# Values turned by VectorE through memory instead of by TensorE, and three small transfers on GpSimd's queue

## The chip, the cores and the metric

The kernel runs on one core of one Trainium2 chip. The metric is device time in microseconds for one execution; the time given for a kernel is the median of its runs. TensorE is called PE in the profile, VectorE DVE, ScalarE ACT, GpSimd POOL, SyncE SP.

## The reference

One step of a small hybrid decoder trunk with two layers. Layer 0 projects 2048 features into the inputs of a gated delta rule (8 heads of 128x128, with a short convolution ahead) and of a gated linear attention, GLA (4 heads, keys of 128, values of 256), and projects their gated outputs back. Layer 1 is a gated linear recurrence (RG-LRU). 256 prompt tokens start from zero state; 64 sample tokens (8 sequences of 8) start from given states. All is float32.

```python
def _ab_mixer(x, S_a, conv_a, S_b, w_in, conv_w, a_log, dt_bias, norm_a, w_lr, b_lr, norm_b, w_out):
    proj = jnp.einsum('btd,de->bte', x, w_in)
    qkv, b_raw, a_raw, z_a, q_b, k_b, v_b, lr_b, z_b = jnp.split(proj, _ab_split_points(), axis=-1)
    qkv, new_conv_a = _causal_conv(qkv, conv_a, conv_w)
    ...
    o_a, S_a_new = _gated_delta_rule(q_a, k_a, v_a, g, beta, S_a)
    ...
    o_b, S_b_new = _gla(q_b, k_b, v_b, gk.reshape(B, T, H_B, DK_B), S_b)
    ...
    return jnp.einsum('bte,ed->btd', o, w_out), S_a_new, new_conv_a, S_b_new

def _gated_delta_rule(q, k, v, g, beta, S0):
    ...
    A = jnp.where(strict, jnp.einsum('nbhid,nbhjd->nbhij', kb, k) * decay, 0.0)
    rhs = jnp.concatenate([v * beta[..., None], kb * jnp.exp(G)[..., None]], axis=-1)
    sol = lax.linalg.triangular_solve(A + jnp.eye(C, dtype=jnp.float32), rhs,
                                      left_side=True, lower=True, unit_diagonal=True)
    ...

def _gla(q, k, v, gk, S0):
    ...
    intra = jnp.einsum('nbhij,nbhjv->nbhiv', A, v)
    def step(S, inp):
        qg_c, k_c, v_c, B_c, intra_c = inp
        o = jnp.einsum('bhck,bhkv->bhcv', qg_c, S) + intra_c
        ...
        S = S * jnp.exp(b_last)[..., None] + jnp.einsum('bhck,bhcv->bhkv', k_dec, v_c)
        return S, o
```

## The kernel before

The projections compute 512 output features at a time: a *group* is 8 weight chunks of 512 KB (tile wst, loaded by SP, line 219), each of two slices of 128 input features. The weights of a slice are split into two float32r parts, wh by ACT (line 253) and wl by DVE (line 254), and each 128x128 block is multiplied in three products of 128x320 (line 386; 320 tokens). A group's four results (f0 to f3) stand in four PSUM banks called acc and are evacuated at its end, mostly by DVE: into slab for the convolved groups (lines 489 and 490, then the taps yc, line 598, and the activation into the tile qkv), into zp and zs for the gates z (lines 1548 and 1549). The next group needs the banks again. The order of groups is Q0, K0, V0, V1, K1, Q1 (delta rule; two halves of four heads), QB, KB, VB0, VB1 (GLA), ZA, ZB, then the output projection (group 14 on) and layer 1.

All other work is written as generators that stand in queues (hi, lo, lo2, tails) and are advanced in *slots* between the products, 64 slots to a group; a table WAITS gives the slots that each generator lets pass at its yields. So the order on every engine is fixed when the kernel is built. A second table, HELD, ties pieces of the GLA sample to chosen products of group 14: key (group, number of the product block), value the pieces held behind it.

V comes out of the projection with features on partitions and is needed with tokens on partitions:

- quad_a prepares a *quad*, four heads of one prompt block of 128 tokens (two halves times two blocks, four prompt quads, and a fifth for the samples). It transposes V on PE (vt, line 791), and the result times bk becomes rv. rv is first used in quad_b, as the right side of the triangular solve. Beside it quad_a makes kt, qt, kk, kq, dtm, bt and mt. delta_half(half) runs quad_a for the two blocks, the inversion of 32x32 blocks, quad_front and quad_b.
- The GLA prompt transposes VB for each block and head, two at a time (gvt, line 1447), together with the keys (line 1448), copies all three to gvk by ACT (line 1450), and uses them in gpo (line 1454) and gsn (line 1458).

delta_sample is one chain for the 8 sequences: own (diagonal 8x8 blocks) is written to memory as bt_scratch (line 808), read as ab (line 857), inverted on DVE by pairs tmp and xi (lines 864 and 866), written to xt_scratch (line 870), read back as own (line 880), spread into XT (line 881) and multiplied with rv to y (line 1085). All four transfers are on SP's queue, between the weight loads. rv of the samples takes the states into account by pq (lines 1069, 1077).

The GLA sample multiplies four 1 MB states (st, loaded at line 1474) in two steps (gpo, line 1517, 32 products on two states each); the tile has three buffers, so the fourth state is loaded once the first step is done.

Of the kernel before, what the change touches and what calls it, by code (L numbers as in the profile page):

```python
# [7 lines left out]
F32 = mybir.dt.float32  # L8
F32R = mybir.dt.float32r
U32 = mybir.dt.uint32  # L10
AF = mybir.ActivationFunctionType
# [3 lines left out]
P = 128  # L15
# [20 lines left out]
NA0 = 2  # L36
# [4 lines left out]
HELD = {(14, 15): (3,), (14, 21): (0, 2), (14, 27): (4,), (14, 33): (1,)}  # L41
# [26 lines left out]
def wait(name):  # L68
    for _ in range(WAITS[name]):
        yield  # L70
# [3 lines left out]
def hybrid_step(ctx, tc, x_cols, x_rows, w_head, w_dense, w_small, w_lr, w_gate, par_a, par_b, par_c, gains, last_gain,  # L74
                head_rows, state_delta, state_gla,
                y_cols, p_delta, p_gla, s_delta, s_gla, dconv, lconv, lru_out):
    nc = tc.nc
# [8 lines left out]
    vk_d = nc.dram_tensor("vk_scratch", (2, 32, 4, 3 * P), F32, kind="Internal").ap()  # L86
    xt_d = nc.dram_tensor("xt_scratch", (4, 16, 8, 8), F32, kind="Internal").ap()
# [10 lines left out]
    def bank4(name):  # L98
        return psum.tile([P, 4, P], F32, name=name, tag="bg", bufs=4)
# [457 lines left out]
    def evac_conv_a(slot_name, half, part):  # L557
# [53 lines left out]
        def after():  # L611
            tails.append(conv_state_out(env["ws"], st["p"], dconv[:, st["ft"]:st["ft"] + 4, :]))
            if part == 2 and half == 0:
                hi.append(later(lambda: lo.append(delta_half(0))))
            if part == 0 and half == 1:
                hi.append(later(lambda: lo.extend([delta_half(1), delta_sample()])))
# [79 lines left out]
    def quad_prompt(half, c):  # L696
        q = Quad()
        q.U, q.n = 4, 32
        q.id = 8 * half + 4 * c
        cs = slice(c * P, (c + 1) * P)  # L700
        q.k = lambda u: env["K", half][:, u, cs]
        q.q = lambda u: env["Q", half][:, u, cs]
        q.v = lambda u: env["V", half][:, u, cs]
        q.qall = lambda: env["Q", half][:, :, cs]
        q.gc = c * 8 + half * 4
        q.um, q.sl, q.far = umask, sl_r, far
        q.late = c > 0
        q.on_tag, q.nbuf = "lg", 2
        return q
# [15 lines left out]
    def quad_a(q, ws, nbuf):  # L725
# [63 lines left out]
        ps = bank4("vt")  # L789
        for u in range(U):  # L790
            pe.transpose(ps[:, u, :], q.v(u), ident)
        q.rv = t("rv")
        scaled4(q.rv, ps, q.bk, NA0)
        yield from wait("quad_a.4")
# [54 lines left out]
    def invert(ws, n_units, n):  # L849
# [7 lines left out]
        sp.dma_start(ab, bt_d.rearrange("u b j i -> (u b) j i"))  # L857
        pool.memset(xi[:parts], 0.0)
        pool.memset(xi[:parts].rearrange("p i c -> p (i c)")[:, ::n + 1], 1.0)
        yield from wait("invert.1")  # L860
# [9 lines left out]
        sp.dma_start(xt_d.rearrange("u b c i -> (u b) c i"), xt)  # L870

    def load_inv(q, ws):
# [4 lines left out]
        else:  # L877
            q.xt = ws.tile([P, 4, P], F32, name="XT", tag="XT")
            own = ws.tile([P, 4, 8], F32, name="own", tag="own", bufs=1)
            q.read = sp.dma_start(own, xt_d.rearrange("u b c i -> (b c) u i"))  # L880
# [116 lines left out]
    def delta_half(half):  # L997
        with tc.tile_pool(name=f"gdn{half}", bufs=1, side="right", reuse_waits="tile") as ws:
# [14 lines left out]
            for p_ in pt:  # L1013
                pool.memset(p_, 0.0)
            yield from wait("quad_b.1")
# [6 lines left out]
    def delta_sample():  # L1022
# [3 lines left out]
        with tc.tile_pool(name="gdns", bufs=1, side="right", reuse_waits="tile") as ws:  # L1026
# [96 lines left out]
            for u in range(4):  # L1123
                to_rows(kt_d[u], q.ktm[:, u, :], P)
        env["done"].add("gdns")

    def to_rows(d, t, w):

        sp.dma_start(bass.AP(tensor=d.tensor, offset=d.offset, ap=[[w, 4], [4 * w, 32], [1, w]]), t)
# [143 lines left out]
    def evac_plain(tag, slot_name, idx, smp, scale=None):  # L1273
# [17 lines left out]
        def after():  # L1291
            env["done"].add((slot_name, idx))
        evac.late = late
        return None, evac, after

# [61 lines left out]
    def gla_head(h, ws, kept):  # L1357
# [74 lines left out]
        for c in range(2):  # L1432
# [12 lines left out]
            for hf in range(2):  # L1445
                vt = 2 * h + hf
                pe.transpose(pt[:, hf, :], env["VB", vt // 4][:, vt % 4, cs], ident)
            pe.transpose(pt[:, 2, :], kd[128][:, cs], ident)
            vk = t("gvk", [P, 3, P])
            act.activation(vk, pt[:, :3], AF.Copy)  # L1450
            yield from wait("gla.3")
            po = bank("gpo")
            vtm = vk[:, 0:2, :].rearrange("p a b -> p (a b)")
# [4 lines left out]
            pe.matmul(ps[:, :256], vk[:, 2, :], vtm, start=True, stop=True)  # L1458
# [670 lines left out]
```

## Time and profile before

| | us |
|---|---|
| median of 3 runs | 967.99 (966.45 to 969.25) |
| the profiled execution | 967.67 |
| its span in the trace | 965.9 |
| granted TensorE clock | 0.999 |
| busy: DVE, ACT, POOL | 684.0, 539.3, 125.6 |

Durations below come from the one profiled execution. A row of a group of instructions gives line, engine, operation, tile written and tiles read, count, and time. Matmuls overlap in the array, so their single durations are longer than the distance between them. In rows of a stretch the engines stand in the order PE, weight loads, DVE, ACT, POOL, with the number of instructions in brackets, then the granted clock, the DMA share and GB/s. In the chain of waits each row is start, duration, what. The DMA moved 175.14 MB, 181 GB/s on average:

```profile
DMA packets 66098, 175.14 MB, mean 181 GB/s; under 512 B 16264, under 2 KB 23688, under 8 KB 65496
q1 hardware_dynamic: 61384, 163.86, 53.2%
q0 software_dynamic: 2560, 8.65, 2.3%
```

q1 carries SP's transfers, q0 those that GpSimd issues.

### The profile page before, as it was taken

To read this page: it belongs to the slowest core of one execution; us is meant where nothing else is said; L and a number is where in the kernel's file an instruction comes from. 1 tells how busy PE (TensorE), PEld (TensorE's weight loads), DVE (VectorE), ACT (ScalarE), POOL (GpSimd) and SP (SyncE) were. 2 spreads that over 40 slices of the span, in tenths; PEclk is the share of its full clock that TensorE was granted. 3 is DMA by queue.
4 is the path that set the end of the run, shared out by engine and by line. 5 is a ranking of instruction groups with operands and counts; after the bars stand their busy time and mean duration, and the time that the engine had idled before them with its cause. 6 is when DMAs were issued, how large, how long until landed. Compare 5 with 4: busy or idle time off the path is not lost.

```text
span 965.9 us, 18747 instructions
## 1 busy us (share of the span) xinstructions
PE 954.4 (99%) x6946; PEld 940.1 (97%) x6946; DVE 684.0 (71%) x1509; ACT 539.3 (56%) x1094; POOL 125.6 (13%) x293
## 2 busy tenths in 40 slices
PE   9999999999999999999999999999999999999997
PEld 9999999999999998999989999999999999999996
DVE  7599887666545566789676778667969668865763
ACT  6767864457333444777434346338696885434452
POOL 3010108303280011121100000100000000000000
PEclk9999999999999999999999999999999999999999
DMA  9854454534554366444568776644436435587742
GB/s 325 286 176 139 134 146 149 151 109 124 156 157 144 108 221 204 159 137 116 211 231 312 239 242 209 226 150 151 157 122 189 132 118 178 191 274 263 252 156 109
DMA packets 66098, 175.14 MB, mean 181 GB/s; under 512 B 16264, under 2 KB 23688, under 8 KB 65496
## 3 DMA queue, kind: packets, MB, share of 16 engines
q1 hardware_dynamic: 61384, 163.86, 53.2%
q0 software_dynamic: 2560, 8.65, 2.3%
q10 hardware_dynamic: 2064, 1.45, 0.5%
q8 instruction: 54, 0.88, 0.4%
q14 instruction: 36, 0.29, 0.1%
HBM read 159.77 MB, written 14.16 MB: 180 GB/s over the span
## 4 chain that ended last, share of the span: by engine, by line
PE 96%; DMA 2%; DVE 1%; issue 0%; ACT 0%; SPq 0%; DVEq 0%
PE acc L386 83%; PE acc L273 3%; DMA st<-in_state_gla_dram 1%; PE fbt L316 1%; PE lg L1709 0%; PE lg L1708 0%; PE lg L1707 0%; PE kq L811 0%; PE kk L797 0%; PE usn L1201 0%; DMA xt_scratch<-ab 0%; PE gpo L1517 0%; PE po L978 0%; PE y L969 0%; DMA wst<-in_w_head_dram 0%; PE sn L983 0%
## 5 line engine op out<-in xcount | busy, mean ns | idle before, releaser
L386 PE MATMUL acc<-xh,wh 128*128 128x320 f32 x1856 | 581.3, 313 | 0.6 <-ACT wh L240 0.6
L386 PE MATMUL acc<-xl,wh 128*128 128x320 f32 x1856 | 574.0, 310 | 0.0
L386 PE MATMUL acc<-xh,wl 128*128 128x320 f32 x1856 | 573.9, 310 | 0.0
L253 ACT ACTIVATE wh<-wst 128x512 fp32r<-128x512 f32 x479 | 279.9, 623 | 300.1 <-PE acc L386 230.7
L254 DVE TENSOR_TENSOR wl<-wst,wh 128x512 fp32r<-128x512 f32 x479 | 317.6, 693 | 166.6 <-ACT wh L253 163.5
L386 PEld LDWEIGHTS acc<-xh,wh 128*128 128x128 f32 x1856 | 348.7, 188 | 3.2 <-issue 0.9
L386 PEld LDWEIGHTS acc<-xl,wh 128*128 128x128 f32 x1856 | 348.6, 188 | 0.5
L386 PEld LDWEIGHTS acc<-xh,wl 128*128 128x128 f32 x1856 | 348.3, 188 | 0.4 <-DVE wl L254 0.3
L598 DVE SCALAR_TENSOR_TENSOR yc<-slab,pa,yc 128x344 f32<-128x344 f32 x72 | 40.8, 579 | 1.7 <-ACT yc L102 1.5
L839 POOL TENSOR_TENSOR tmp<-ab,xi 128x60 f32<-128x60 f32 (+24 forms) x62 | 23.9, 386 | 55.7 <-DMA ab<-bd_scratch 51.1
L841 POOL TENSOR_TENSOR xi<-xi,tmp 128x60 f32<-128x60 f32 (+24 forms) x62 | 25.5, 411 | 4.9
L1231 POOL DMA_DIRECT2D out_s_delta_dram<-ust x8 | 5.9, 742 | 102.8 <-DVE ust L1228 102.8
L1265 POOL DMA_DIRECT2D out_s_gla_dram<-ugt x8 | 4.3, 542 | 113.5 <-DVE ugt L1262 113.5
L273 PE MATMUL acc<-xl,wh 128*128 128x320 f32 (+1 forms) x64 | 18.7, 292 | 0.0
L273 PE MATMUL acc<-xh,wl 128*128 128x320 f32 (+1 forms) x64 | 18.7, 292 | 0.0
L273 PE MATMUL acc<-xh,wh 128*128 128x320 f32 (+1 forms) x64 | 18.6, 291 | 0.0
L602 ACT ACTIVATE qkv<-yc 128x256 f32<-128x256 f32 x24 | 9.9, 414 | 15.2 <-DVE yc L598 15.2
L1228 DVE SCALAR_TENSOR_TENSOR ust<-ust,es,usn 128x128 f32<-128x128 f32 x64 | 18.3, 345 | 0.1
L1667 DVE SCALAR_TENSOR_TENSOR yc<-slab,pb,yc 128x344 f32<-128x344 f32 x32 | 17.4, 576 | 0.7 <-ACT yc L1665 0.5
L489 DVE TENSOR_TENSOR slab<-acc,rb 128x256 f32<-128x256 f32 x36 | 15.0, 418 | 3.3 <-PE acc L386 3.0
L1736 POOL MEMSET aa<- 128x32 f32 x4 | 0.7, 166 | 120.9 <-ACT rr L1723 66.2
L102 ACT ACTIVATE yc<-slab,pa 128x344 f32<-128x344 f32 x24 | 13.7, 577 | 4.8 <-DVE slab L490 4.5
(468 smaller groups left out, 990.2 us busy)
## 6 DMA issues: line engine op xcount, KB each, us to landing
wst<-in_w_dense_dram SPq DMA_DIRECT2D x237, 512.0 KB, 3.7
st<-in_state_delta_dram SPq DMA_DIRECT2D x8, 512.0 KB, 5.8
st<-in_state_gla_dram SPq DMA_DIRECT2D x4, 1024.0 KB, 5.8
ust<-in_state_delta_dram SPq DMA_DIRECT2D x8, 512.0 KB, 5.9
out_s_delta_dram<-ust POOLq DMA_DIRECT2D x8, 512.0 KB, 6.5
ugt<-in_state_gla_dram SPq DMA_DIRECT2D x8, 512.0 KB, 5.0
out_s_gla_dram<-ugt POOLq DMA_DIRECT2D x8, 512.0 KB, 4.1
xtok<-in_x_rows_dram SPq DMA_DIRECT2D x6, 512.0 KB, 7.3
```

What stands on the lines that cost most here:

```text
L102: return act.activation(out, in_, AF.Identity, scale=scale)
L253: act.activation(h, wst[i][:, a, :], AF.Copy)
L254: env["last_split"] = dve.tensor_sub(l, wst[i][:, a, :], h.bitcast(F32))
L273: mm = pe.matmul(accs[f][:, cols], w[:, fs], x[:, cols], start=(k == 0 and j == 0), stop=(k == KT - 1 and j == 2), skip_group_check=True)
L386: mm = pe.matmul(o, (h, h, l)[j][:, fs], (xh, xl, xh)[j][k], start=(k == 0 and j == 0), stop=(k == KT - 1 and j == 2))
L489: dve.tensor_mul(xp[:, 3:259], xp[:, 3:259] if acc is None else acc[:, :256], rb[:, :256])
L598: dve.scalar_tensor_tensor(y[:, :n], xp[:, j:j + n], pa[:, ft, j:j + 1], y[:, :n], op0=OP.mult, op1=OP.add)
L602: act.activation(st["t"][:, f, :], y[:, :TP], AF.Silu)
L839: behind(pool.tensor_mul(tv, ab[:, j, j + 1:, None].to_broadcast([P, m, w]), xi[:, j:j + 1, :w].to_broadcast([P, m, w])))
L841: behind(pool.tensor_add(xi[:, j + 1:, :w], xi[:, j + 1:, :w], tv))
L1228: dve.scalar_tensor_tensor(s_, s_, es[:, col:col + 1], ps[b][:, r, :], op0=OP.mult, op1=OP.add)
L1667: dve.scalar_tensor_tensor(y[:, :n], xp[:, j:j + n], pb[:, ft, 2 + j:3 + j], y[:, :n], op0=OP.mult, op1=OP.add)
```

## The change

Four things change.

1. V of both halves and VB of both halves are turned by a new generator, turn: four DVE stream transposes (of 32x32 blocks) into the buffer ob[3], one write of 512 KB to vt_scratch, two reads of 256 KB back into the tile that V came from, all on SP. turned gives the view of the result, in which the 256 or 512 numbers of a token lie in runs of 32. The prompt quads make rv in delta_half just ahead of quad_front, after waiting for the flag ("V", half); the samples keep their PE transposes. The GLA reads VB through the same view, and ACT copies only the keys.
2. The read of bt_scratch, the write of xt_scratch and the read of own in delta_sample are issued by GpSimd; the write of bt_scratch stays on SP. The kt_scratch writes are ordered behind the read of own.
3. In HELD the first GLA sample step (piece 3) and the preparation of the second (pieces 0 and 2) are tied to product blocks four earlier, which is 12 products; the second step (piece 4) stays.
4. delta_half(0) starts some slots later, since the entry that starts turn stands ahead of it in hi.

```diff
-HELD = {(14, 15): (3,), (14, 21): (0, 2), (14, 27): (4,), (14, 33): (1,)}
+HELD = {(14, 11): (3,), (14, 17): (0, 2), (14, 27): (4,), (14, 33): (1,)}
...
-    "tables.2": 14, "small_work.4": 3, "small_work.5": 9, "gla_decays.8": 11, "quad_b.9": 1,
+    "tables.2": 14, "turn.1": 3, "turn.2": 4, "turn.3": 14, "turn.4": 31, "small_work.4": 3, "small_work.5": 9, "gla_decays.8": 11, "quad_b.9": 1,
...
+    vt_d = nc.dram_tensor("vt_scratch", (4, 2, P, 4 * P), F32, kind="Internal").ap()
...
+            if part == 2:
+                hi.append(later(lambda: lo2.append(turn(st["t"], st["t"], 2 + half, ("V", half), True))))
...
-        q.v = lambda u: env["V", half][:, u, cs]
+        q.v = lambda: turned(env["V", half], c)
...
-        ps = bank4("vt")
-        for u in range(U):
-            pe.transpose(ps[:, u, :], q.v(u), ident)
-        q.rv = t("rv")
-        scaled4(q.rv, ps, q.bk, NA0)
-        yield from wait("quad_a.4")
+        if q.n == 8:
+            ps = bank4("vt")
+            for u in range(U):
+                pe.transpose(ps[:, u, :], q.v(u), ident)
+            q.rv = t("rv")
+            scaled4(q.rv, ps, q.bk, NA0)
+            yield from wait("quad_a.4")
...
-        sp.dma_start(ab, bt_d.rearrange("u b j i -> (u b) j i"))
+        pool.dma_start(ab, bt_d.rearrange("u b j i -> (u b) j i"))
...
-        sp.dma_start(xt_d.rearrange("u b c i -> (u b) c i"), xt)
+        pool.dma_start(xt_d.rearrange("u b c i -> (u b) c i"), xt)
...
-            q.read = sp.dma_start(own, xt_d.rearrange("u b c i -> (b c) u i"))
+            q.read = pool.dma_start(own, xt_d.rearrange("u b c i -> (b c) u i"))
...
+            while ("V", half) not in env["done"]:
+                yield
+            for q in qs:
+                q.rv = ws.tile([P, 4, P], F32, name="rv", tag="rv", bufs=2)
+                by = q.rv.rearrange("p u (a j) -> p u a j", a=4)
+                for u in range(2):
+                    scaled(by[:, u], q.v()[:, u], q.bk[:, u:u + 1])
+                dve.tensor_mul(by[:, 2:], q.v()[:, 2:], q.bk[:, 2:, None, None].to_broadcast([P, 2, 4, 32]))
...
-                to_rows(kt_d[u], q.ktm[:, u, :], P)
+                order(to_rows(kt_d[u], q.ktm[:, u, :], P), q.read)
-        sp.dma_start(bass.AP(tensor=d.tensor, offset=d.offset, ap=[[w, 4], [4 * w, 32], [1, w]]), t)
+        return sp.dma_start(bass.AP(tensor=d.tensor, offset=d.offset, ap=[[w, 4], [4 * w, 32], [1, w]]), t)
...
-            env["done"].add((slot_name, idx))
+            if slot_name == "VB":
+                lo2.append(turn(st["t"], st["t"], idx, (slot_name, idx)))
+            else:
+                env["done"].add((slot_name, idx))
+    def turn(t, out, idx, flag, pause=False):
+        if pause:
+            yield from wait("turn.4")
+        to = ob[3].rearrange("p f t -> p (f t)")[:, :8 * P].rearrange("p (c b u j) -> p u c b j", c=2, u=4, j=32)
+        for f in range(4):
+            yield from wait("turn.1")
+            behind(dve.transpose(to[:, f], t[:, f, :].rearrange("p (c i b) -> p c b i", c=2, b=4)))
+        yield from wait("turn.2")
+        behind(sp.dma_start(vt_d[idx].rearrange("c p x -> p c x"),
+                            ob[3].rearrange("p f t -> p (f t)")[:, :8 * P].rearrange("p (c x) -> p c x", c=2)))
+        yield from wait("turn.3")
+        rows = out.rearrange("p f t -> p (f t)")[:, :8 * P].rearrange("p (c a x) -> p c a x", c=2, a=4)
+        for c in range(2):
+            behind(sp.dma_start(rows[:, c], vt_d[idx, c].rearrange("(a i) (b x) -> (i b) a x", a=4, b=4)))
+            yield from wait("turn.1")
+        env["done"].add(flag)
+    def turned(t, c):
+        return t.rearrange("p f t -> p (f t)")[:, 4 * c * P:4 * (c + 1) * P].rearrange(
+            "p (a u j) -> p u a j", a=4, u=4)
...
-            for hf in range(2):
-                vt = 2 * h + hf
-                pe.transpose(pt[:, hf, :], env["VB", vt // 4][:, vt % 4, cs], ident)
-            pe.transpose(pt[:, 2, :], kd[128][:, cs], ident)
-            vk = t("gvk", [P, 3, P])
-            act.activation(vk, pt[:, :3], AF.Copy)
+            pe.transpose(pt[:, 0, :], kd[128][:, cs], ident)
+            kt = t("gkt", [P, P])
+            act.activation(kt, pt[:, 0], AF.Copy)
-            vtm = vk[:, 0:2, :].rearrange("p a b -> p (a b)")
+            vtm = turned(env["VB", h // 2], c)[:, 2 * (h % 2):2 * (h % 2) + 2]
-            pe.matmul(ps[:, :256], vk[:, 2, :], vtm, start=True, stop=True)
+            pe.matmul(ps[:, :256], kt, vtm, start=True, stop=True)
```

**The sample inversion on DVE.** Before, the last rows of DVE ahead of y: zp and zs are the evacuation of f3 of group ZA, rv takes in pq, wl is a weight split.

```order
448 L1548 TENSOR_TENSOR zp<-acc,rb_84 128x256
449 L1549 TENSOR_TENSOR zs_234<-acc,rb_84 128x64
450 L1077 SCALAR_TENSOR_TENSOR rv<-pq,nbe_4708,rv 128x128 x2
451 L254 TENSOR_TENSOR wl<-wst,wh 128x512
452 L1077 SCALAR_TENSOR_TENSOR rv<-pq,nbe_4708,rv 128x128
453 L881 TENSOR_TENSOR XT<-own,u8mask 128x512
```

The same place of the changed kernel:

```order
477 L1089 SCALAR_TENSOR_TENSOR rv<-pq,nbe_4716,rv 128x128
478 L885 TENSOR_TENSOR XT<-own,u8mask 128x512
479 L1583 TENSOR_TENSOR zp<-acc,rb_84 128x256
480 L1584 TENSOR_TENSOR zs_234<-acc,rb_84 128x64
481 L1089 SCALAR_TENSOR_TENSOR rv<-pq,nbe_4716,rv 128x128 x2
482 L255 TENSOR_TENSOR wl<-wst,wh 128x512
483 L1089 SCALAR_TENSOR_TENSOR rv<-pq,nbe_4716,rv 128x128
```

XT, which waits for own, has moved from behind these rows to ahead of the evacuation and of three of rv's four updates. The pairs of the inversion (tmp and xi), between which zp evacuations of f0 to f2 stood, now follow each other, with the evacuations behind the copy that ends them.

**The same on the queues.** Before, SP's queue from the second kt write to own:

```order
81 L1129 DMA kt_scratch<-ktm 4x32x128 x2
82 L808 DMA bt_scratch<-own 128x4x8
83 L1129 DMA kt_scratch<-ktm 4x32x128
84 L219 DMA wst<-in_w_dense_dram 128x1024
85 L857 DMA ab<-bt_scratch 64x64
86 L219 DMA wst<-in_w_dense_dram 128x1024 x2
87 L870 DMA xt_scratch<-ab 64x64
88 L880 DMA own<-xt_scratch 128x4x8
89 L1035 DMA st<-in_state_delta_dram 128x1024 x4
```

The changed kernel's SP queue there (gp is VB1, read back from vt_scratch):

```order
88 L1325 DMA gp<-vt_scratch 128x4x128
89 L220 DMA wst<-in_w_dense_dram 128x1024
90 L1325 DMA gp<-vt_scratch 128x4x128
91 L220 DMA wst<-in_w_dense_dram 128x1024
92 L812 DMA bt_scratch<-own 128x4x8
93 L220 DMA wst<-in_w_dense_dram 128x1024 x3
94 L1141 DMA kt_scratch<-ktm 4x32x128 x2
95 L1047 DMA st<-in_state_delta_dram 128x1024 x4
```

And its GpSimd (qm is the keys' operand for pq):

```order
200 L1073 COPY qm<-smpK 128x8x8 x4
201 L863 DMA ab<-bt_scratch 64x64
202 L874 DMA xt_scratch<-ab 64x64
203 L884 DMA own<-xt_scratch 128x4x8
204 L1073 COPY qm<-smpK 128x8x8 x4
205 L1114 TENSOR_TENSOR so<-so,mhalf 128x4
```

Three transfers have left SP for GpSimd, where they stand between the two sets of qm copies; a weight load stands on SP ahead of bt where two kt writes were.

**VectorE behind V0.** The changed kernel, after the evacuation of group V0 (qkv is V0, ob_142 the buffer ob[3]; yc are taps; dtm, bt and mt belong to quad_a of half 0):

```order
236 L1318 STREAM_TRANSPOSE ob_142<-qkv 128x8x32
237 L599 SCALAR_TENSOR_TENSOR yc<-slab,pa,yc 128x344
238 L781 TENSOR_TENSOR dtm<-dtm,nb 128x512
239 L1318 STREAM_TRANSPOSE ob_142<-qkv 128x8x32
240 L803 TENSOR_TENSOR bt<-kk,dtm 128x512
241 L818 TENSOR_TENSOR mt<-kq,dtm 128x512
242 L1318 STREAM_TRANSPOSE ob_142<-qkv 128x8x32
243 L255 TENSOR_TENSOR wl<-wst,wh 128x512
244 L1318 STREAM_TRANSPOSE ob_142<-qkv 128x8x32
245 L599 SCALAR_TENSOR_TENSOR yc<-slab,pa,yc 128x344
```

The four transposes of a turn stand among taps, weight splits and the quad's own products; before, dtm and bt of this quad stood ahead of the slab evacuations of the group, mt behind the first of them, and none of the transposes was there.

## The prediction

> **What bounds the kernel now.** I read the page first (busy time, then the chain that ended last), then TensorE's waits, then busy time by stretch.
>
> ```profile
> PE 954.4 (99%) x6946; PEld 940.1 (97%) x6946; DVE 684.0 (71%) x1509; ACT 539.3 (56%) x1094; POOL 125.6 (13%) x293
> PE 96%; DMA 2%; DVE 1%; issue 0%; ACT 0%; SPq 0%; DVEq 0%
> ```
>
> TensorE (PE) is busy for 99% of the 965.9 us span and owns 96% of the chain of waits. So a PE instruction that goes is worth its whole time, provided that nothing it fed comes late; and PE's few idle moments are all that else can be won.
>
> ```profile
> PE y L1085 <- DVE XT L881: 1.5, 1, 1.5
> ...
> PE gpo L1517 <- DMA st<-in_state_gla_dram: 1.4, 1, 1.4
> ...
> 352.00:372.00 20.00, 18.51 (x177) 17.86 (x177) 14.70 (x48) 8.53 (x13) 1.25 (x4) 1.00 0.50 152
> ...
> 475.00:500.00 25.00, 23.65 (x199) 21.41 (x198) 17.01 (x40) 9.26 (x17) 1.75 (x6) 1.00 0.70 249
> 500.00:950.00 450.00, 450.00 (x3150) 447.57 (x3149) 328.56 (x634) 249.75 (x417) 15.54 (x33) 1.00 0.60 196
> ```
>
> Two idle moments concern the change: 1.5 us before y of the delta sample (its 20 us stretch holds 18.51 busy) and 1.4 us before gpo of the GLA sample (23.65 of 25). From 500 to 950 us PE is full.
>
> **1. Transposes that leave PE.**
>
> ```profile
> 112.30 6.60 PE acc L386 x45
> ...
> 119.37 0.44 PE vt L791 x4
> ...
> L1447 PE MATMUL gvt<-ident,gp x16: 272/273/273, 413.8 to 461.4; 128*128 128x128 f32 x16
> ...
> 425.70 0.38 PE L1447 MATMUL gvt<-ident,gp 128*128 128x128 f32 x2
> 425.91 0.27 PE L1448 MATMUL gvt<-ident,k 128*128 128x128 f32 x1
> ```
>
> The 272 ns of one is its latency; matmuls are pipelined, so the price is the distance between starts. On the chain four vt take 0.44 us, 0.11 each (and 45 of the projections' products 6.60, 0.147 each); in PE's timeline two gvt stand between 425.70 and 425.91, 0.105 each. The change removes 16 vt (four prompt quads) and 16 gvt (16 rows above): 4 x 0.44 + 8 x 0.21 = 3.4 us. **Term 1: -3.4.**
>
> The GLA products gpo and gsn (32 of 128x256) then read V with a stride, in runs of 32 numbers. No row shows such a read at this size. The nearest:
>
> ```profile
> 372.55 0.86 PE pq L1092 x4
> ...
> 413.14 0.33 PE L1436 MATMUL ga<-q,kn 128*128 128x64 f32 x2
> 413.30 0.39 PE L1436 MATMUL ga<-q,k 128*128 128x64 f32 x2
> ```
>
> A contiguous read of 128 columns takes 0.11 us (vt, above); pq reads a 128-wide piece twice, 256 columns in 0.86/4 = 0.215, so leaving the straight row cost it nothing. The other end is ga, which reads runs of 16: 0.08 us (413.14 to 413.30, two) for 64 columns, where half of vt's is 0.055; if the whole excess were the stride, 256 columns would cost 0.1 more, 32 of them 3.2 us. But ga also changes weights every 64 columns, which explains it as well. I take 0, by pq, which is as wide; bounds 0 and +3.2.
>
> **2. The work VectorE (DVE) and the DMA queues get.**
>
> ```profile
> L927 DVE STREAM_TRANSPOSE xz<-xc x2: 434/434/435, 193.0 to 303.9; 32x256 f32<-32x256 f32 x2
> ...
> 124.00:136.00 12.00, 12.00 (x87) 12.00 (x87) 10.81 (x27) 7.41 (x14) 0.00 (x0) 1.00 0.30 70
> 136.00:150.00 14.00, 14.00 (x98) 14.00 (x97) 9.64 (x17) 7.63 (x18) 5.05 (x14) 1.00 0.77 217
> ...
> L1139 SPq DMA_DIRECT2D uk<-kt_scratch x4: 525/525/614, 492.8 to 567.7; - x4
> ...
> DMA to landing us min/median/max: 3.8/4.9/6.1
> ```
>
> Sixteen stream transposes with 256 numbers in each partition, 0.43 us by the L927 row (32 partitions there, 128 here): 6.9 us of DVE. The multiplications of rv stay on their engines, ScalarE loses two thirds of the gvk copies. The tightest place is the seam of V0 and the next group, where delta_half(0) also starts 7 slots (about 3 us) later: 124 to 150 us has 26 - 10.81 - 9.64 = 5.55 us idle and receives 4 x 0.43 = 1.7. It fits on average, so I cost it at 0; if the late quad work lands right among the slab evacuations, those 1.7 us, or the whole 3.1 us of the shift, come to PE as late weights or a late PSUM bank. Bounds 0 and +3.1. Each turn also queues a 512 KB write and two 256 KB reads on SP between the weight loads. A read back of that size landed in 6.1 us at most (uk, above). The reads are issued about 58 products of 0.147 us ahead of the evacuation that stands behind rv on DVE, 8.5 us; so 2.4 us remain. Cost 0.
>
> **3. The GLA sample, moved 12 products earlier.**
>
> ```profile
> 482.98 1.86 PE gpo L1517 x32
> ...
> 484.90 7.83 DMA st<-in_state_gla_dram
> ...
> 492.87 1.93 PE gpo L1517 x32
> ...
> 479.03 5.76 SPq L219 DMA_DIRECT2D wst<-in_w_dense_dram  x3
> ```
>
> The fourth state is loaded into the buffer that the first gpo frees, and the second gpo waits for it. With the first gpo 12 products earlier (12 x 0.147 = 1.76 us) and the second where it was, the load starts 1.76 us earlier, behind two weight loads in place of three. The wait is 1.4: it goes, with 0.36 us to spare. **Term 2: -1.4**; bounds -1.4 and 0 (if the load, at 7.83 us already long, takes 1.4 more).
>
> **4. The inversion's transfers on GpSimd's queue.**
>
> ```profile
> 352.43 3.07 DMA bt_scratch<-own
> 355.52 2.81 DMA ab<-bt_scratch
> 358.35 0.17 DVE tmp L864
> ...
> 361.82 0.33 DVE zp L1548
> 362.16 0.13 DVE zs L1549
> ...
> 363.33 0.17 DVE ab L868
> 363.52 3.93 DMA xt_scratch<-ab
> 367.51 1.80 DMA own<-xt_scratch
> 369.34 0.70 DVE XT L881
> ...
> bd_scratch<-bt SPq DMA_DIRECT2D x16, 16.0 KB, 2.1
> xd_scratch<-xt POOLq DMA_DIRECT2D x8, 32.0 KB, 3.7
> ...
> L846 POOL DMA_DIRECT2D xd_scratch<-xt x8: 596/634/847, 176.3 to 288.9; - x8
> ...
> DMA to landing us min/median/max: 1.9/3.7/4.4
> ```
>
> In before's clock: the write of bt no longer stands behind kt writes, so 2.1 (bd_scratch) in place of 3.07: it lands at 354.5. Then ab by GpSimd, at L846's median: 358.2. DVE's part took 363.50 - 358.35 = 5.15 us, with three zp evacuations between the pairs, 3 x (0.33 + 0.13) = 1.4, that now stand behind the copy to ab: 3.75, to 361.95. Then xt and own, 3.7 each: 369.35. Before, own landed at 367.51 + 1.80 = 369.31, so **the chain itself comes out even**. By the fastest L846 landings (1.9 each) own lands at 363.95, by the slowest (4.4) at 371.45.
>
> What changes is who waits behind. XT (0.70) now stands on DVE ahead of the last zp evacuation (0.33 + 0.13), which frees a bank that PE needs three products before y, and ahead of three of rv's four updates. I add that evacuation: **term 3: +0.5**; bounds -1.5 (the wait vanishes) and +2.6 (own at 371.45: 2.1 later, and the 0.5). Behind own on GpSimd stand four qm copies, whose product is some 12 us away; behind it on SP the kt writes and the second pair of states, which have about as long.
>
> [...]
>
> **Sum**, against the profiled execution's 967.67 us (span 965.9 and 1.8 around it; the median, 967.99, is 0.3 higher): -3.4 - 1.4 + 0.5 = -4.3, so **963.4 us**.
>
> **Rivals.**
>
> *Quick queue.* GpSimd's transfers land like L846's fastest, own at 363.95, XT is done well before y, the 1.5 us wait goes: -3.4 - 1.4 - 1.5 = -6.3, 961.4 us. For it: 16 KB is half of L846's transfer, and no weights stand in that queue. Against: the median.
>
> *Late own.* Landings of 4.4: +2.6 for term 3, so -3.4 - 1.4 + 2.6 = -2.2: 965.5 us. For it: three transfers in a row, each issued by an engine that takes 596 to 847 ns to do so.
>
> *Crowded VectorE.* At the seam after V0, +1.7 to +3.1 on the forecast: 965.1 to 966.5 us. For it: 10.81 us of 12 busy. Against: 4.4 us idle in the next 14. The strided read ends in the same place (963.4 + 3.2 = 966.6 at its bound).
>
> [...]
>
> *Late read back.* If V0 lands later than the 8.5 us, rv holds DVE, and with it the slab evacuations; a loss only from 4.3 us beyond that, 12.8 us after the issue, where a 1 MB state took 7.83.
>
> *Only the transposes.* The moved parts change nothing: 967.67 - 3.4 = 964.3, inside the forecast's own band.
>
> **How the numbers follow.** Forecast 963.4 (band 962.2 to 964.8) 0.45; quick queue 0.19; late own 0.14; crowded VectorE or stride 0.12; starved queue 0.07; late read back 0.03. The range takes the first three whole and most of the fourth: 960.9 to 966.6. A measurement of this kernel tells about 0.3% (2.9 us) from no change, so faster means below 965.1: forecast and quick queue, 0.64, and a little of the crowded case: 0.65. Same, up to 970.9: 0.25. Slower: the starved queue and the late read back, 0.10.
>
> **What would show it.** PE's count falls by 32 and its busy time by 3.4 us; the wait of gpo for st is gone; y's wait for XT between 0 and 4 us, with DVE's idle time before XT put down to own. The landings on GpSimd's queue decide term 3: at 1.9 the quick case, at 4.4 or more the late one. A wait of PE for a slab or wl near 125 to 150 us is the crowded case; rv or DVE waiting for vt_scratch the late read back; gpo and gsn starts 0.3 us apart the stride. I am wrong if PE waits at a place named nowhere here.

## The result, and the profile after

The changed kernel is slower: 975.95 us (median of 4 runs, 973.63 to 976.61) against 967.74 (4 runs), a ratio of 1.008 with a 95% interval of 1.006 to 1.0101. Its profiled execution took 973.63 us, span 971.7: 6.0 more than the profiled execution before, where the medians differ by 8.2. It is the fastest of the four; the other three show a mean granted clock of 0.993 to 0.995 against its 0.996, so the sums below, taken from its trace, leave 2.2 us out.

The page of the changed kernel, busy time and the chain that ended last:

```profile
PE 954.7 (98%) x6914; PEld 938.9 (97%) x6914; DVE 692.5 (71%) x1525; ACT 539.5 (56%) x1096; POOL 127.5 (13%) x296
PE 88%; POOL 4%; DMA 2%; DVE 2%; issue 2%; ACT 1%; SPq 1%; DVEq 0%; POOLq 0%
```

32 PE instructions are gone, as announced, and PE's busy time hasn't fallen: something made the others longer. And 8% of the chain has left PE, half of it for GpSimd, which had no share before. PE's waits in the changed kernel (total, times, longest):

```profile
PE acc L387 <- DVE zs L1584: 3.2, 1, 3.2
PE lp L927 <- DVE xz L921: 2.2, 1, 2.2
...
PE gr L770 <- DVE ug L761: 1.0, 1, 1.0
PE y L973 <- issue: 0.7, 1, 0.7
...
PE y L1097 <- DVE rv L1089: 0.4, 1, 0.4
PE kq L815 <- DVE bt L803: 0.4, 1, 0.4
```

The wait of gpo is gone. The wait of y for XT has become one of the projection for a gate evacuation (zs). Four new waits belong to the delta rule's prompt quads: lp and y (L973) to half 0's triangular solve, gr and kq to half 1's quad_a.

Where it went, exactly: both kernels run the same 5568 products of 128x320 in the same order, so the start of the n-th in one trace against the other tells what happened up to it.

| product | start before | start after | difference | what lies between |
|---|---|---|---|---|
| 640 | 104.38 | 104.82 | +0.44 | the head (the clock's first rise: 4.2 us before, 5.3 after) |
| 1170 | 189.23 | 188.79 | -0.44 | 8 vt of half 0 gone: -0.88 |
| 1330 | 226.28 | 229.50 | +3.23 | half 0's solve: +3.67 |
| 1500 | 257.46 | 262.28 | +4.82 | half 1's quad_a: +1.59, with 8 vt gone |
| 2100 | 361.51 | 366.35 | +4.84 | nothing |
| 2180 | 378.38 | 387.03 | +8.65 | the delta sample: +3.81 |
| 2670 | 472.36 | 479.52 | +7.16 | 16 gvt gone: -1.49 |
| 2800 | 499.60 | 505.41 | +5.81 | gpo's wait gone: -1.35 |
| 5567 | 926.23 | 932.10 | +5.87 | nothing |

**The delta sample.** The chain of the changed kernel, PE's granted clock behind it (stretches; the clock stands third from the end), and what SP issued beside own:

```profile
368.99 5.84 DMA own<-xt_scratch
...
374.85 0.69 DVE XT L885
375.54 0.34 DVE zp L1583
...
377.43 0.80 PE y L1097 x2
378.23 2.97 PE acc L387 x12
```

```profile
376.00:378.00 2.00, 1.46 (x8) 1.30 (x8) 2.00 (x7) 1.48 (x2) 0.00 (x0) 0.84 0.68 272
378.00:380.00 2.00, 2.00 (x10) 2.00 (x9) 2.00 (x5) 0.94 (x2) 0.00 (x0) 0.50 0.77 238
380.00:382.00 2.00, 2.00 (x11) 1.90 (x10) 0.52 (x1) 0.00 (x0) 0.00 (x0) 0.80 0.42 91
```

```profile
369.06 1.89 SPq L1047 DMA_DIRECT2D st<-in_state_delta_dram  x4
```

Own took 5.84 us where it took 1.80, with 2 MB of states issued 0.07 us behind it. Before, those states stood behind own in SP's queue, and their first packets of 4 KB started at 369.05, where own's last had started at 368.97; in the changed kernel nothing but the order in which the planner (the step that builds the kernel) put the issues has them behind. Yet own landed only 0.7 us later, because it was issued earlier: less the 4.84 us by which the changed kernel stands behind at product 2100, it was issued at 364.15 in place of 367.51 and landed at 369.99 in place of 369.31. The rest of the delay stands behind XT on VectorE: the evacuation, and ahead of y three updates of rv and a weight split.

Then the clock: 12 products that took 1.75 us before take 2.97, because the clock is at half for 3.4 us after PE's 3.2 us of idleness. From product 2100 to 2180, in the kernel before and in the changed one (length, then PE's busy time and instructions):

```profile
361.51:378.38 16.87, 15.38 (x154) 14.63 (x153) 11.16 (x33) 8.31 (x19) 2.64 (x7) 1.00 0.63 221
```

```profile
366.35:387.03 20.68, 17.13 (x154) 16.21 (x153) 11.21 (x32) 8.32 (x19) 3.52 (x9) 0.92 0.63 199
```

Of the 3.81 us, PE waits for 2.06 and is busy longer, at the lower clock, for 1.75. The latter is about half of the busy time that didn't fall; the rest is 1.0 in half 1's quads, 0.4 in half 0's solve and 0.5 in the head. Before, 1.5 us of idleness left the clock at 1.00:

```profile
370.00:372.00 2.00, 1.92 (x14) 1.92 (x15) 2.00 (x4) 0.63 (x1) 0.00 (x0) 1.00 0.94 344
```

In runs below the clock fell to 0.50 behind shorter waits of PE too, of 2.2, 2.0 and 1.6 us.

**Half 0.** The second bt of half 0, on VectorE's timeline in the kernel before and in the changed one:

```profile
126.47 0.69 DVE L799 TENSOR_TENSOR bt<-kk,dtm 128x512 f32<-128x512 f32 x1
```

```profile
136.18 0.65 DVE L803 TENSOR_TENSOR bt<-kk,dtm 128x512 f32<-128x512 f32 x1
```

It is the last input of the inversion on GpSimd, 60 us ahead of lp. It came 9.7 us later, because the quad's work now stands behind the evacuations, taps and transposes of the group's end. The inversion, before and in the changed kernel, began 5.3 us later:

```profile
143.93 0.24 POOL L839 TENSOR_TENSOR tmp<-ab,xi 128x31 f32<-128x31 f32 x1 [26.41 <-DMA ab<-bd_scratch]
```

```profile
149.27 0.24 POOL L843 TENSOR_TENSOR tmp<-ab,xi 128x31 f32<-128x31 f32 x1 [29.16 <-DMA ab<-bd_scratch]
```

Its result was written to xd_scratch at 181.75 in place of 176.35, read back, and transposed to xz, for which lp waits. lp began at 194.67 in place of 190.82, so 3.85 us of that were left, more than the chain had to spare: PE waited 2.2.

**Half 1.** ScalarE and VectorE of the changed kernel, with the idle time before an instruction and its releaser in brackets:

```profile
233.31 0.40 ACT L103 ACTIVATE rv<-qkv,bk 128x128 f32<-128x128 f32 x1 [1.29 <-POOL bk L754]
...
237.53 0.40 ACT L103 ACTIVATE rv<-qkv,bk 128x128 f32<-128x128 f32 x1 [1.46 <-POOL bk L754]
```

```profile
237.53 0.42 DVE L1026 TENSOR_TENSOR rv<-qkv,bk 128x256 f32<-128x256 f32 x1 [1.45 <-POOL bk L754]
```

The program text puts rv behind the inversion, some 60 us later (291.76 in e7_both below, where it is tied to that place). Half 1's V has been read back long before, and the program's order doesn't hold rv to its place, so the planner lifted it up to the squares of kt and qt, where both engines wait in order for GpSimd's bk, and the squares, weight splits and ug behind them are late.

### The profile page after: what moved, and what is told of

It reads as the page before. It is cut to its first block, busy times and chain, and to the rows that moved or that the text cites. A ratio compares the mean times of both kernels' runs of the same rounds, so it can differ in the third digit from the quotient of the medians.

```text
span 971.7 us, 18713 instructions
## 1 busy us (share of the span) xinstructions
PE 954.7 (98%) x6914; PEld 938.9 (97%) x6914; DVE 692.5 (71%) x1525; ACT 539.5 (56%) x1096; POOL 127.5 (13%) x296
## 4 chain that ended last, share of the span: by engine, by line
PE 88%; POOL 4%; DMA 2%; DVE 2%; issue 2%; ACT 1%; SPq 1%; DVEq 0%; POOLq 0%
PE acc L387 76%; PE acc L274 3%; POOL xi L845 1%; POOL tmp L843 1%; DVE wl L255 1%; DMA own<-xt_scratch 1%; PE fbt L317 1%; PE lg L1744 0%; PE lg L1743 0%; PE lg L1742 0%; DMA wst<-in_w_head_dram 0%; PE usn L1213 0%; DMA ab<-bd_scratch 0%; PE y L973 0%; PE kk L801 0%
```

## The experiments

Fifteen kernels, each compared by its median with the kernel before on the same chip; the ratio has its 95% interval.

| run | median | before | ratio |
|---|---|---|---|
| e1_sp | 973.23 | 966.98 | 1.0065 (1.0042 to 1.0088) |
| e2_gp | 972.05 | 966.98 | 1.0059 (1.0042 to 1.0076) |
| e3_vb | 966.16 | 966.98 | 0.9992 (0.9981 to 1.0002) |
| e4_v | 972.76 | 966.98 | 1.0060 (1.0045 to 1.0075) |
| e5_pin | 970.33 | 967.93 | 1.0024 (1.0013 to 1.0035) |
| e6_first | 968.98 | 967.93 | 1.0009 (0.9998 to 1.0021) |
| e7_both | 966.43 | 967.93 | 0.9986 (0.9976 to 0.9996) |
| e8_states | 971.54 | 967.93 | 1.0040 (1.0026 to 1.0055) |
| e9_alone | 969.65 | 966.24 | 1.0029 (1.0014 to 1.0043) |
| e10_before_y | 964.87 | 966.24 | 0.9984 (0.9972 to 0.9996) |
| e11_both_y | 963.12 | 966.24 | 0.9965 (0.9953 to 0.9977) |
| e12_own_sp | 968.95 | 967.36 | 1.0022 (1.0008 to 1.0036) |
| e13_gp_xt | 968.91 | 967.98 | 1.0016 (1.0002 to 1.0031) |
| e14_sp_xt | 967.23 | 967.98 | 0.9993 (0.9980 to 1.0005) |
| e15_xt_first | 967.82 | 967.98 | 1.0003 (0.9990 to 1.0017) |

### One part at a time

e1_sp, the changed kernel without the GpSimd queue:

```diff
-        pool.dma_start(ab, bt_d.rearrange("u b j i -> (u b) j i"))
+        sp.dma_start(ab, bt_d.rearrange("u b j i -> (u b) j i"))
...
-        pool.dma_start(xt_d.rearrange("u b c i -> (u b) c i"), xt)
+        sp.dma_start(xt_d.rearrange("u b c i -> (u b) c i"), xt)
...
-            q.read = pool.dma_start(own, xt_d.rearrange("u b c i -> (b c) u i"))
+            q.read = sp.dma_start(own, xt_d.rearrange("u b c i -> (b c) u i"))
...
-                order(to_rows(kt_d[u], q.ktm[:, u, :], P), q.read)
+                to_rows(kt_d[u], q.ktm[:, u, :], P)
```

> The changed kernel with the three transfers of the sample inversion back on SyncE's queue (and the kt writes in their old place); all else as changed. Theory A (three separate sums: the transposes and the GLA sample save, the GpSimd queue costs about 3.8 us net, the delta rule's V costs about 4.5 us net): y waits 1 to 2 us again, no wait for zs, no half clock behind it, so about 3.8 us less than the changed kernel, 970 to 972. Rival B (the queue is a bystander, the chain was late because everything ahead of it was): stays within 1 us of the changed kernel, 975.

e2_gp is the kernel before with these lines the other way round.

> The kernel before with only the three transfers moved to GpSimd's queue. Theory A: own is issued beside the second pair of states, lands 4 to 6 us after its issue instead of 1.8, VectorE stands at XT with the last gate evacuation behind it, TensorE waits 3 us or more and then runs at a lower clock for some us: 970 to 972, that is +3 to +4. Rival B (harmless without the delta rule's delay): 966 to 968. Rival C (the queue helps by itself, as my quick case had it): 966.

e3_vb is e1_sp with V turned by PE again in quad_a and no turn in the delta rule; e4_v is e1_sp with gvt of two halves, gvk and HELD as before.

> The kernel before with only the GLA's values VB turned by VectorE and with the new HELD; V and the queues as before. Theory A: 16 transposes (1.7 us) and the wait of gpo (1.4 us) go, nothing else moves: 964 to 965.3. Rival: the strided read or the extra VectorE work costs it back, 967 or more.

> The kernel before with only the delta rule's V of both halves turned by VectorE; VB, HELD and the queues as before. Theory A: 16 transposes (1.75 us) go, but the second bt of half 0 comes some 10 us later, the inversion on GpSimd with it, so lp waits about 2 us, and the early rv of half 1 holds ScalarE and VectorE for GpSimd's bk, so gr and kq wait about 1.4 us more: 971 to 973. Rival: V alone is a saving and only the sum of all edits is late: 966.

Both large costs stood up by themselves: e2_gp lost 5.1 us and e4_v 5.8, a little more than theory A gave. The wait of e2_gp, and the clock 2 us behind it:

```profile
PE acc L386 <- DVE zs L1549: 3.5, 1, 3.5
...
374.00:376.00 2.00, 2.00 (x9) 2.00 (x9) 2.00 (x5) 0.94 (x2) 0.00 (x0) 0.50 0.58 215
```

It is the changed kernel's, without any of its other edits: the queue is no bystander. e1_sp's profiled execution (970.27) was where theory A put it, its median 1.2 us above that range. By the medians the changed kernel wins less from losing the queue than by the traces: 1.0065 in place of 1.0080, with intervals that overlap (1.0042 to 1.0088, 1.0060 to 1.0101). The parts don't add up by the medians either: 5.1 + 5.8 - 0.8 is 10.1, where the whole change lost 8.2. e3_vb fell short: 0.8 us won by the median (its interval takes in no change) and 1.9 by the profiled execution, where 3.1 were expected. Its trace has the 3.07 us by product 2800, then gives 0.9 back in one wait for a weight near product 2880, at 510.00; what makes that weight late wasn't followed:

```profile
PE acc L387 <- ACT wh L254: 0.8, 1, 0.8
```

### The two halves of the delta rule

e5_pin ties rv to its place in the text; e6_first swaps the entries; e7_both does both. All start from e1_sp.

```diff
-                    scaled(by[:, u], q.v()[:, u], q.bk[:, u:u + 1])
-                dve.tensor_mul(by[:, 2:], q.v()[:, 2:], q.bk[:, 2:, None, None].to_broadcast([P, 2, 4, 32]))
+                    behind(scaled(by[:, u], q.v()[:, u], q.bk[:, u:u + 1]))
+                behind(dve.tensor_mul(by[:, 2:], q.v()[:, 2:], q.bk[:, 2:, None, None].to_broadcast([P, 2, 4, 32])))
```

```diff
-            if part == 2:
-                hi.append(later(lambda: lo2.append(turn(st["t"], st["t"], 2 + half, ("V", half), True))))
             if part == 2 and half == 0:
                 hi.append(later(lambda: lo.append(delta_half(0))))
+            if part == 2:
+                hi.append(later(lambda: lo2.append(turn(st["t"], st["t"], 2 + half, ("V", half), True))))
```

> The kernel of e1_sp (all edits but the GpSimd queue) with the four multiplications of rv tied to their place in the program, behind the product ahead of them, so that those of half 1 no longer stand between the squares of kt and qt. Theory A (half 1's loss is ScalarE and VectorE waiting in order for GpSimd's bk ahead of work that the next products need): the waits of gr and kq in 240 to 247 us go, about 3 us less than e1_sp's profiled 970.3: 967 to 968, while lp near 194 us still waits 2.3. Rival (half 1 is late only because half 0 was): no change against e1_sp.

> The kernel of e1_sp with the two entries in hi swapped, so that delta_half(0) starts where it did in the kernel before and the turn of V0 comes after it. Theory A (half 0's loss is the late second bt, behind slab evacuations, taps and transposes, and the late inversion behind it): bt is back near 126 us, lp doesn't wait, about 3 us less than e1_sp's profiled 970.3: 967 to 968, while gr and kq still wait. Rival (the transposes and the read back themselves crowd half 0): lp still waits 1 us or more.

> Both of e5_pin and e6_first. Theory A: the two losses are separate and both go, 6 us less than e1_sp's profiled 970.3: 963.5 to 965.5, below the kernel before by the 32 transposes and gpo's wait, less about 0.9 for a late weight near 510 us. Rival: one hides the other, 967 or more.

The two losses are separate. Pinning rv alone took the waits of gr and kq away and left lp's 2.6 us; starting half 0 early alone cut lp's wait to 0.6 and left gr's 1.0; both together left 0.2 of lp's and nothing of gr's. In e7_both product 1330 starts 0.69 us ahead of the kernel before and product 1500 1.57, so both lots of eight vt are won, and 0.2 us of them is given back at lp. The medians follow: 1.0065, then 1.0024, 1.0009, and 0.9986 with both. In e5_pin and in e4_v the late inversion has a second victim: a copy into the slab that stands behind it on GpSimd (L518), for which VectorE waits with an evacuation, and PE then 1.2 us for that one. In e4_v:

```profile
187.26 0.43 DVE L490 TENSOR_TENSOR slab<-acc,rb 128x256 f32<-128x256 f32 x1 [2.50 <-POOL slab L518]
```

e7_both's profiled execution took 963.96, as expected, but its median is 2.5 us above, and its wait of y for XT is 1.8 us. e6_first's profile shows what can happen in an execution, PE's wait and the clock behind it:

```profile
372.49 0.71 PE L1097 MATMUL y<-rv,XT 128*128 128x128 f32 x4 [2.17 <-DVE XT L885]
...
375.00:377.00 2.00, 2.00 (x7) 1.64 (x7) 0.44 (x1) 0.00 (x0) 0.00 (x0) 0.50 1.01 408
```

Here the clock fell behind 2.17 us of idleness, 1.0 us less than in the changed kernel.

### Own, its queue and XT's place

e8_states is e2_gp with the second pair of states on GpSimd's queue behind own; e9_alone is e2_gp with that pair issued by SP behind y and a further weight load.

```diff
-                    i = sp.dma_start(st[:, e], state_delta[2 * u + e])
+                    i = (pool if u > 1 else sp).dma_start(st[:, e], state_delta[2 * u + e])
```

```diff
-                if pr == 0:
-                    load(2)
-                    load(3)
                 yield from wait("delta_sample.4")
                 ps = bank4("y0")
...
+                if pr == 0:
+                    load(2)
+                    load(3)
                 y0 = t("y0", [P, 2, P])
```

> The kernel of e2_gp (before with only the three transfers on GpSimd's queue) with the second pair of delta states issued by GpSimd too, behind own, in place of SyncE. Theory A (own lands late because 2 MB of states, no longer behind it in one queue, share the DMA engines with it): own lands 2 to 3.5 us after its issue in place of 5 to 6, no wait for zs, TensorE's clock stays at 1.00: 966.5 to 968.5. Rival (GpSimd's queue is slow by itself): own still takes 5 us or more, 971 to 972.

> The kernel of e2_gp (before with only the three transfers on GpSimd's queue) with the second pair of delta states issued by SyncE behind y and behind one more weight load, so that nothing but weight loads moves while own is read. Theory A, sharpened by e8_states (own at 4.6 us with the states behind it on GpSimd): sharing is most of it, own lands 2 to 3.5 us after its issue, the wait of zs is under 0.5 us and the clock stays at 1.00: 966.5 to 968.5. Rival (GpSimd's queue is slow by itself): own takes 4.5 us or more, 971.

Theory A fell in part: own took 4.6 us in e8_states, and still 4.4 in e9_alone, with no states beside it. GpSimd's issue of it and VectorE's wait in e9_alone:

```profile
364.20 0.82 POOL L880 DMA_DIRECT2D own<-xt_scratch  x1 [1.46 <-PE pq L1069]
```

```profile
368.59 0.69 DVE L881 TENSOR_TENSOR XT<-own,u8mask 128x512 f32<-128x512 f32 x1 [3.29 <-DMA own<-xt_scratch]
```

So the states explain some 1.5 us of own's 5.8, not most of it. But own wasn't alone in e9_alone either: SP issued the four kt writes from 362.91 on, and from 366 to 368 the DMA moved 93 GB/s, where it moved 41 while own was read in the kernel before. e12_own_sp keeps ab and xt_scratch on GpSimd and puts own on SP, ahead of the states.

> The kernel of e2_gp with only the read of own back on SyncE's queue, ahead of the second pair of states there (and the kt writes as before); the read of ab and the write of xt_scratch stay on GpSimd, and XT stays ahead of the last gate evacuation on VectorE. Theory D, after e9_alone (own took 4.4 us on GpSimd beside nearly idle DMA engines, so its queue is slow for this read by itself, and the states add 1.5): own lands about 2 us after its issue near 364.3, XT is done by 367.5, neither zs nor y makes TensorE wait, 1.5 us less than the kernel before, 965 to 966.3. Rival (the place of XT in VectorE's order makes the wait, whoever reads own): 969 or more.

It lost too. On SP, read 3 us earlier than before and soon behind a weight load, own took 4.0 us:

```profile
364.28 4.03 DMA own<-xt_scratch
...
368.34 0.69 DVE XT L881
369.03 0.33 DVE zp L1548
369.36 0.13 DVE zs L1549
369.49 0.52 DVE rv L1077 x2
370.01 0.60 DVE wl L254
370.61 0.27 DVE rv L1077
...
370.93 0.49 PE y L1085 x2
```

XT began 1.0 us earlier than before, and the second pair of y's products 0.85 us later: what VectorE had finished ahead of XT before (the evacuation, three rv and a weight split) now follows it. PE's waits are only 0.46 us longer for it (1.95 from product 2100 to 2180, 1.49 before), but the clock fell to half near 371.6 (0.91 from 370 to 372, 0.50 from 372 to 374), and product 2180 starts 2.2 us later. The last three kernels separate this order from the queue. In e13_gp_xt (from e2_gp) and e14_sp_xt (from e12_own_sp) XT is emitted just ahead of y, so that VectorE's order is the old one; e15_xt_first is the kernel before with only the gate evacuation ordered behind XT.

```diff
                 yield from wait("delta_sample.4")
+                if pr == 0:
+                    q.spread()
                 ps = bank4("y0")
```

```diff
-            dve.tensor_mul(zp[:, f, :], acc[:, :TP], rb0[:, :TP])
+            i = dve.tensor_mul(zp[:, f, :], acc[:, :TP], rb0[:, :TP])
+            if idx == 0 and f == 3:
+                order(i, env["xt"])
```

> The kernel of e2_gp (before with only the three transfers on GpSimd's queue) with XT back behind the last gate evacuation and rv, so that VectorE's order there is that of the kernel before. Theory Q (the queue costs by the late landing of own): own still takes 5 to 6 us beside the states, lands near 370, so y waits about 2.5 us and the clock falls behind it: 968.5 to 971. Theory P (the place of XT is the cost, by holding a PSUM bank): no wait above 1 us, 966 to 967.5.

> The kernel of e12_own_sp (ab and xt_scratch on GpSimd, own on SyncE) with XT back behind the last gate evacuation and rv. Own lands about 4 us after 364.3 as in e12_own_sp, XT is done at 369.1, y is due at 368.6. Theory P: y waits about 0.5 us and the clock stays, 966 to 967, a little below before and 2 to 3 us below e12_own_sp. Theory Q (where XT stands doesn't matter, only when own lands): as e12_own_sp, 968 to 969.

> The kernel before, all on SyncE's queue, with the last gate evacuation put behind XT on VectorE. Own lands at 369.3 as before, XT ends at 370.0, the evacuation at 370.5, and the bank is due at 368.0. Theory P: TensorE waits about 2.4 us in place of 1.5 and the clock falls behind it: 969 to 970.5. Theory Q: no change, within 1 us of before.

With XT in its old place the queue costs 0.16% in place of 0.59%, and own's SP variant wins 0.07% (its interval takes in 0) in place of losing 0.22%. So the order makes most of the loss; by theory P, though, e13_gp_xt should have had no wait, and own took 6.29 us there and y waited 2.4, as theory Q had it. And the evacuation alone behind XT cost nothing (e15_xt_first), against theory P; in its profiled execution own landed at 367.7, and PE had no wait to speak of. Each alone costs at most 0.31% by its interval; the late own and the work put behind it cost 0.4 to 0.8% together. The order costs 0.22 and 0.29% where own even lands earlier than before, by 1.0 us in e12_own_sp and 0.7 in e9_alone. Of own's lateness a part goes with GpSimd's queue and a part with the traffic beside it (last section); how much each makes, no run shows by itself.

y of e13_gp_xt waited 2.4 us without the clock falling behind it; e2_gp's wait was followed by half clock, so the gap between these two kernels is in part that of the clock:

```profile
372.00:374.00 2.00, 2.00 (x16) 1.92 (x14) 2.00 (x5) 0.00 (x0) 0.00 (x0) 1.00 0.96 391
```

### A version that beats both

e10_before_y is the kernel before with y and its successors 18 products later; e11_both_y is e7_both with the same.

```diff
                 yield from wait("delta_sample.4")
+                if pr == 0:
+                    for _ in range(6):
+                        yield
```

> The kernel before with y of the first sample pair, and what follows it, 18 products (2.6 us) later. Theory: the 1.5 us wait for XT is filled with products, nothing else moves: 1.5 us less than before, 966.2 by the profiled execution. Rival (the later chain makes pq of the second pair or a weight split late): no change.

> The kernel of e7_both with the same shift of y. Theory: the wait for XT (1.8 us in e7_both's profile, and by the lower clocks of its other executions often long enough there to halve the clock) is gone: profiled 962, a median of 962 to 964 with the executions closer together, 4 to 5 us below the kernel before. Rival (the spread of e7_both has another cause): median stays at 966.

Both came out as expected, but for e11_both_y's distance to the kernel before, 3.1 us and not 4 to 5. e11_both_y, which holds the turned V and VB, the new HELD, early half 0, pinned rv and the later y, with the sample's transfers on SP, takes 963.12 us against 966.24, 0.35% less; e10_before_y alone gives 0.16%. The other 1.8 us by the medians (3.7 by the profiled executions, 962.28 against 965.97) are what comes out of the 3.4 us of transposes and of gpo's wait. PE's longest waits in e11_both_y:

```profile
PE frs L359 <- DVE rr L357: 1.4, 1, 1.4
PE warm L1900 <- DVE mhalf L1884: 1.1, 1, 1.1
PE lp L927 <- DVE xz L921: 0.2, 1, 0.2
```

The first two are the kernel's tail and head; between them hardly a wait is left. The twelve executions of e10_before_y lie within 1.7 us, the 29 of the kernel before beside them within 5.7: so much of the spread goes with that wait.

## Why the prediction was wrong

The forecast was 963.4 us with a range to 966.6; the kernel took 975.95, 8.2 more than before. Step by step:

- **Term 1, transposes (-3.4): right.** 0.88 for each half (e7_both) and 1.49 to 1.76 for the GLA (product 2380 to 2670 in the changed kernel and in e7_both). The strided read costs nothing that shows, as taken.
- **Term 2, gpo (-1.4): the mechanism was right**, 1.35 here: none of the seven traces with the new HELD has that wait. Its size is that of one execution: in the ten traces with the old HELD the wait was 1.8 us twice, 1.2 to 1.4 three times, 0.9, 0.6 and 0.2 once each, and absent in e12_own_sp and e14_sp_xt, 0.9 on average.
- **Step 2, the work on VectorE, costed at 0 with bounds 0 and +3.1: this step failed.** It cost 3.67 us in half 0 and 1.59 + 0.88 = 2.47 in half 1, 6.1 together. I looked for the price where the work is, at the seam near 125 to 150 us, as late weights or a late bank, and found that it fits on average. It does: PE didn't wait there. The price fell due 60 us later, at lp, at the end of a chain over GpSimd and memory that began with the bt that I had pushed back. For half 1 the prediction says that the multiplications of rv stay on their engines; they do, but ahead of work that the next products need, behind a wait for bk. The orders printed ahead of the prediction showed bt among the transposes; that I didn't follow it to lp is the error. The waits of lp, gr and kq are at places that the prediction names nowhere, its own sign of being wrong.
- **Term 3, the GpSimd queue (+0.5, bounds -1.5 and +2.6): the sign was right, the size wrong**: 3.81 by the traces, 5.1 by e2_gp's median. That the chain itself came out nearly even, with own 0.7 us later, was luck: own was priced by L846 (3.7, at most 4.4) and took 5.84, but the write of xt_scratch, priced the same, took 1.7. Of the states and kt writes on SP I asked only whether they would be late, not what they would do to own. Of what stands behind XT I added the evacuation (0.46), but not rv and the weight split (1.39 us on the chain, for which PE waited 0.4), nor that the bank is needed three products (0.44) before y. And no price was put on the clock, 1.75 us, nearly half of the loss.
- **Sum**: -3.4 - 1.4 + 0.5 against, between the products of the table, -0.88 + 3.67 + 1.59 + 3.81 - 1.49 - 1.35 = +5.4. With the head and the tail that is the 6.0 us between the profiled executions. The other 2.2 us of the medians' 8.2 stand in no trace. One half-clock stretch of 3.4 us lowers the mean clock by 0.0018, so the other executions' 0.993 to 0.995 would be about one or two stretches more, an estimate of 1.7 us each.
- **Rivals.** The late own happened, above its price for that read and below it for the landing. The crowded VectorE happened, by another way than the one named. The late read back and the stride didn't: nothing in the changed kernel's trace waits for vt_scratch, and the GLA's stretch became shorter by what the transposes are worth. A starved queue, in which GpSimd's transfers wait for VectorE (0.07 in the chances), is shown by no run: VectorE stood idle for the last 4.7 of own's 5.84 us.

## What to carry to other kernels

An engine with idle time to spare says nothing of an instruction that starts a long chain: follow the first moved result to its last reader, and to what stands behind its chain on each engine, and compare there with what the chain had to spare. An instruction that waits for a transfer is priced with everything that stands behind it on its engine; and a transfer that leaves a queue can lose the order that it had there (own ran ahead of the states before, beside them in the changed kernel), so ask what now runs beside it. An instruction moved in the text of a planned kernel stays where it is put only if it is tied there.

## What the runs showed of the hardware

An idle gap of PE cost more than its length in five traces: the granted clock stood at 0.50 for 3.4 us behind a wait of PE of 3.2 us (the changed kernel), 3.5 (e2_gp), 2.2 (e6_first), 2.0 (e8_states) and 1.6 (e12_own_sp). In the changed kernel PE was busy 1.75 us longer for it. Behind 1.5 us (before), 1.6 (e1_sp), 1.7 (e9_alone), 1.8 (e7_both) and 2.4 us (e13_gp_xt) the clock stayed at 1.00. So the length of the wait alone doesn't decide, and what does was not shown. The shortest wait that half clock followed and the longest that it didn't follow (e12_own_sp, then e13_gp_xt):

```profile
368.00:370.00 2.00, 0.44 (x3) 0.39 (x3) 1.66 (x6) 0.60 (x1) 0.00 (x0) 1.00 0.98 383
370.00:372.00 2.00, 1.62 (x12) 1.43 (x11) 2.00 (x5) 1.17 (x3) 0.00 (x0) 0.91 1.04 408
372.00:374.00 2.00, 2.00 (x9) 2.00 (x9) 2.00 (x5) 0.74 (x2) 0.00 (x0) 0.50 0.84 326
```

```profile
368.00:370.00 2.00, 1.23 (x9) 0.96 (x7) 0.00 (x0) 1.80 (x4) 0.00 (x0) 1.00 1.03 319
370.00:372.00 2.00, 0.42 (x3) 0.42 (x4) 1.17 (x2) 0.00 (x0) 0.00 (x0) 1.00 0.99 393
372.00:374.00 2.00, 2.00 (x16) 1.92 (x14) 2.00 (x5) 0.00 (x0) 0.00 (x0) 1.00 0.96 391
```

How long own, a read of 16 KB, took went with what the DMA moved meanwhile, and with the queue. On SP it took 1.8 us beside 41 GB/s (before), 3.5 in e14_sp_xt (264 GB/s from 364 to 366, 199 from 366 to 368) and 4.0 in e12_own_sp (187 from 366 to 368, 383 from 368 to 370). On GpSimd's queue it took 4.4 us in e9_alone (93 from 366 to 368, 34 from 368 to 370), 4.6 in e8_states (288 from 366 to 370), 5.8 in the changed kernel (276 while it ran), 5.9 in e2_gp and 6.3 in e13_gp_xt (230 from 366 to 368, 319 from 368 to 370). So e9_alone's read took 0.4 us longer on GpSimd's queue than e12_own_sp's on SP beside more traffic from 366 on, one trace each. The packets show where: the first started 1.0 us after the issue on SP (before) and 3.2 us after it on GpSimd's queue (the changed kernel).

The stream transposes over 128 partitions took 0.63 us each by the trace's group in the changed kernel, half as long again as the row over 32 partitions that I had taken (0.43):

```profile
L1318 DVE STREAM_TRANSPOSE ob<-qkv x8: 624/633/643, 134.0 to 171.2; 128x256 f32<-128x256 f32 x8
```
